# A two-layer decoder step: memory attention ahead of the HGRN heads, both sample heads of a pair in one step, twelve gates behind them

## The chip, the cores and the metric

One Trainium2 chip, one of its cores. TensorE (PE in the profile), VectorE (DVE), ScalarE (ACT), GpSimd (POOL) and the DMA queues run in parallel, each engine in its own order, and wait for each other by semaphores. The metric is the device time of one execution in microseconds (us); lower is better. The time before the change is the median of three runs.

## What is computed

264 tokens (256 of a prompt, 8 samples that each have caches of their own) go through two layers of width 2048. The second layer, where nearly all of the change lies, is this, cut from the reference:

```python
q, f, iv, mq, g = split(x @ w_in)              # 12 + 12 + 12 + 4 + 16 blocks of 128 columns
fg = lb + (1 - lb) * sigmoid(f)                # forget gate
qh, kh, vh = silu(q), 1 - fg, iv
# per head: prompt in chunks, each sample with its own state
state = fg * state + outer(kh, vh);  o = qh @ state
o = o * rsqrt(mean(o**2) + eps) * norm_w
mem = softmax(mq @ mem_k.T / sqrt(128)) @ mem_v    # 4 heads; samples use cache_mem_k, cache_mem_v
y = (concat(o, mem) * silu(g)) @ w_out
x = layer_norm(alpha * x + y)
```

The first layer has sliding-window attention in place of the twelve recurrent heads, and the same memory heads, gates, output projection and norm.

## The kernel before

**The stream.** All that is read in large pieces goes through one list of units (`Stream`, L58 to L131). A unit is a weight block of 128 output columns, or a cache or state block; nearly all are 128 partitions by 2048 numbers in float32, 1 MB. For each unit SyncE (SP) issues a load into one of 4 raw tiles; ACT writes the high float16 half of each number (L97) and DVE the low half, the rest (L98), into one of 4 tiles `hl`; then the unit's function runs. Up to 4 units are split ahead. A raw tile comes free when it has been split; a state tile (`whole=True`) stays, since the new state is computed in it and stored from it.

**A projection** (`proj`, L307) is 48 matmuls: 16 chunks c of the contraction, each in three passes (`passes`, L302 to L305): high weight by high input, high by low, low by high. Each has 264 columns. They add up in one PSUM bank of the tag `pj`, of which there are two; two banks each exist of `pt` and `sc`, one each of `pv` and `ms`.

**Side work.** The attention of a head and the chunkwise recurrence of a pair of heads (`hg_side`, L1064) are generators in a queue. After each unit `after` (L1278) calls `pump(1)`: the first generator in the queue runs one step. For a pair the steps are: diagonal products `hd`; products for the spans 1, 2, 4, 8, 16, 32, 64 (`hs`, masked into `st`); transposes `pk` and updates `pu`; the output `hpo`; square and mean (`rms`, L1182); log and exponential (L1183, L1186) for the reciprocal root; the scaled result (L1189). What is written here is the order of issue; a scheduler then sets each engine's order by a model of its own, so that side work stands between the matmuls of projections. At run time every engine keeps that order.

**Layer two**, as it stands in the list: for each of six pairs of heads the blocks f, f, v, v, q, state, q, state, where a state unit is one head (half a tile, L1197 to L1243: sample output `hos`, then eight updates of the state by ACT L1237 and DVE L1238, each with a product `vb` from PE, then a store from POOL's queue, L1241). For heads 0 to 7 (`NG1`) the gate block g comes right behind its state unit. Then four blocks mq, four blocks of the memory key cache and four of the value cache (`ck_unit`, `cv_unit`, each 32 very small matmuls, with the softmax `mems_soft` between them), gates 8 to 15 among and behind them, then the 16 blocks of the output projection (`o`). A gate unit (`gate_unit`) computes silu; `gate_by` (L727) multiplies it into the head's result and splits the product into the tile `mix`, chunk j, which is what the output projection reads. The output projection's first unit first drains the side queue (`out_unit`, L767).

In the first layer the first q block follows the block of keys and values `kv`, which holds both `pj` banks (and both `sc`) until L249, L251 and their neighbours have read them; in the same way the first f block of layer two follows `mv`.

Of the kernel before, what the change touches and what calls it, by code (L numbers as in the profile page):

```python
# [18 lines left out]
P = 128  # L19
# [14 lines left out]
NG1 = 8  # L34
# [23 lines left out]
class Stream:  # L58


    def __init__(self, nc, pool, nraw, nsplit):
        self.nc, self.pool = nc, pool
        self.nraw, self.nsplit = nraw, nsplit
        self.units = []
        self.raw = {}
        self.hl = {}

# [16 lines left out]
    def prep(self, i):  # L84
# [9 lines left out]
        for k, s in enumerate(self.parts(i)):  # L94
# [10 lines left out]
    def run(self, pump):  # L105
# [11 lines left out]
        for i in range(n):  # L117
# [8 lines left out]
            while free < prepped and (free <= i or self.units[free][5]):  # L126
                free += 1
# [7 lines left out]
def trunk_kernel(  # L135
# [75 lines left out]
    bias_s = pm.tile([P, 2, NQ], F32, name="bias_s")  # L211

# [770 lines left out]
    def f_unit(h):  # L983
        def fn(hl):
# [4 lines left out]
            pt = proj(hl, xhl, T, f"f{h}")  # L989
            i = h % 2  # L990
            if i == 0:
# [3 lines left out]
                cur["ks8"] = p1.tile([P, 2, TS], F32, tag="ks8", name=f"ks8{h}", bufs=2)  # L995
            fg, kk, ks8 = cur["fg"][:, i], cur["kk"][:, i], cur["ks8"][:, i]
# [6 lines left out]
            nc.vector.tensor_scalar_mul(ks8, kk, 1.0 / (SA * SK))  # L1003
# [5 lines left out]
    def hq_unit(h):  # L1009
        def fn(hl):  # L1010
# [5 lines left out]
            if h % 2 == 1:  # L1016
                side.append(hg_side(h // 2, cur["q"], cur["vn"], cur["fg"], cur["qk"]))
# [23 lines left out]
    def hv_rows(h, vt, vs, vn, vr):  # L1041
# [7 lines left out]
        nc.vector.tensor_copy(vr[:, i], p16)  # L1049
# [14 lines left out]
    def hg_side(pi, q, vn, fg, qk):  # L1064
# [119 lines left out]
        for i, sq in enumerate(sqs):  # L1184
# [3 lines left out]
            scaled = mix[:, h] if h >= NG1 else sq  # L1188
# [3 lines left out]
            if h < NG1:  # L1192
                gate_by(sq, mix[:, h], h)
# [3 lines left out]
    def state_unit(h):  # L1197
        def fn(hl):
            p1 = H["p"]
            pi, i = h // 2, h % 2  # L1200
            raw = stream.raw[state_at[h]][:, : TS * P]
            R = raw.rearrange("p (b v) -> p b v", b=TS)
            v = hl[:, :, : TS * P].rearrange("p s (b v) -> p s b v", b=TS)
            vr, fgs, ks8 = cur["vr"][:, i], cur["fg"][:, i, TP:T], cur["ks8"][:, i]
            qs, vts = (cur[n][:, i, TP:T] for n in ("q", "vt"))
            ks = cur["kk"][:, i]
            if i == 0:
                osb[pi] = p1.tile([P, 2, T], F32, tag="osb", name=f"osb{pi}", bufs=2)
            qk = p1.tile([P, TS], F32, tag="qk", name=f"qk{h}", bufs=2)
            qf = p1.tile([P, TS], F32, tag="qf", name=f"qf{h}", bufs=2)  # L1210
            qfh = p1.tile([P, TS, 2], F16, tag="qfh", name=f"qfh{h}", bufs=2)
            nc.vector.scalar_tensor_tensor(qf, qs, SA * 0.5 * CP, fgs, op0=ALU.mult, op1=ALU.mult)
            nc.vector.scalar_tensor_tensor(qk, qs, 8.0 * 0.5 * CP / SK, ks, op0=ALU.mult, op1=ALU.mult)
            qkh = p1.tile([P, 2, TS], F16, tag="qkh", name=f"qkh{h}", bufs=2)
            nc.scalar.activation(qkh[:, 0], qk, AF.Copy)
            nc.vector.tensor_tensor(qkh[:, 1], qk, qkh[:, 0], op=ALU.subtract)
            nc.scalar.activation(qfh[:, :, 0], qf, AF.Copy)
            nc.vector.tensor_tensor(qfh[:, :, 1], qf, qfh[:, :, 0], op=ALU.subtract)
            po = bank("ms", 1, f"hos{h}")
            pov = po[:, : 2 * TS].rearrange("p (b s) -> p b s", s=2)  # L1220
            for b in range(TS):
                mm(pov[:, b], v[:, 0, b], qfh[:, b], start=True, stop=False)
                mm(pov[:, b, 0:1], v[:, 1, b], qfh[:, b, 0:1], start=False, stop=True)
# [49 lines left out]
    while late:  # L1273
        g1(late.popleft())
# [158 lines left out]
```

## Time and profile before

| | us |
|---|---|
| median of three runs | 906.5 (905.1 to 909.17) |
| the profiled execution | 906.08 |
| its span, first to last instruction | 904.3 |
| PE busy in the span | 886.6 |
| DVE busy | 701.5 |
| ACT busy | 582.4 |

Layer two's f block begins at 420.1 us of the span, its caches at 729 us, its output projection at 800 us. In the rows of the profile, a line such as `PE hpo L1169 <- ACT st L1147: 1.5, 1, 1.5` says that PE, about to run the instruction of line 1169 that writes `hpo`, stood idle for 1.5 us, once, until ACT had done line 1147, which writes `st`. In a table of windows each engine's number is its busy time in that stretch, with the number of its instructions; PEclk is the granted TensorE clock, 1.00 being full. A matmul's time in the timeline holds its way through the array: two of them overlap, so that matmuls of 264 columns start 0.11 us apart and each lasts 0.28.

### The profile page before, as it was taken

What the parts mean: (1) busy time and instruction counts of PE and PEld (TensorE: products, weight loads), DVE (VectorE), ACT (ScalarE), POOL (GpSimd) and SP (SyncE); (2) the same over time, 40 slices, a digit from 0 to 9 for tenths busy, and PEclk for the clock granted to TensorE, in tenths of its full rate; (3) what the DMA queues carried; (4) which work ended last, traced back from release to release, by engine and by line L of the source; (5) the groups of instructions that cost most, each with busy time, mean ns of one, the idle gap of its engine ahead of it and who ended that gap; (6) DMA issues with size and microseconds to landing.
All of it is one profiled execution on the core that took longest, in us unless ns stands there. A gap on an engine that the chain in (4) does not pass through costs nothing.

```text
span 904.3 us, 21814 instructions
## 1 busy us (share of the span) xinstructions
PE 886.6 (98%) x9281; PEld 762.9 (84%) x9281; DVE 701.5 (78%) x1230; ACT 582.4 (64%) x982; POOL 34.9 (4%) x68
## 2 busy tenths in 40 slices
PE   9999999999999999999999999999999999799996
PEld 6888889678888888876888888898888888688996
DVE  6879877669886666697687887979788989678736
ACT  6767776657664444476766877777777585858415
POOL 1100010000000000002000000000000000000000
PEclk9999999999999999999999999999999999899999
DMA  9998566557785555556374655827454878456303
GB/s 340 392 353 317 188 245 209 188 208 265 262 333 192 187 192 203 207 198 214 127 292 137 216 201 174 299 101 260 160 215 164 303 283 308 172 207 244 130 2 97
DMA packets 37853, 198.67 MB, mean 220 GB/s; under 512 B 4555, under 2 KB 10732, under 8 KB 17532
## 3 DMA queue, kind: packets, MB, share of 16 engines
q1 hardware_dynamic: 33024, 181.55, 56.3%
q0 software_dynamic: 4688, 15.67, 4.6%
q8 instruction: 72, 1.18, 0.5%
q14 instruction: 25, 0.20, 0.1%
q10 hardware_dynamic: 44, 0.07, 0.0%
HBM read 180.03 MB, written 17.22 MB: 218 GB/s over the span
## 4 chain that ended last, share of the span: by engine, by line
PE 77%; DVE 8%; ACT 6%; DMA 6%; issue 3%; SPq 0%; ACTq 0%; DVEq 0%
PE o L303 5%; PE o L305 5%; PE o L304 5%; PE g L305 5%; PE g L303 5%; PE g L304 5%; DVE hl L98 4%; ACT hl L97 2%; PE hv L305 2%; PE hv L303 2%; PE hv L304 2%; DMA raw<-in_w_in 2%; PE hq L303 2%; PE hq L305 2%; PE hq L304 2%
## 5 line engine op out<-in xcount | busy, mean ns | idle before, releaser
L98 DVE SCALAR_TENSOR_TENSOR hl<-raw,hl 128x2048 f16<-128x2048 f32 (+2 forms) x168 | 358.6, 2138 | 82.0 <-ACT hl L97 81.0
L97 ACT ACTIVATE hl<-raw 128x2048 f16<-128x2048 f32 (+2 forms) x168 | 299.2, 1784 | 97.8 <-PE o L305 45.4
L305 PEld LDWEIGHTS <-hl 128*128 128x128 f16 (+2 forms) x2048 | 197.4, 98 | 31.8 <-DVE hl L98 2.9
L303 PEld LDWEIGHTS <-hl 128*128 128x128 f16 (+2 forms) x2048 | 197.3, 98 | 30.6 <-issue 2.2
L304 PEld LDWEIGHTS <-hl 128*128 128x128 f16 (+2 forms) x2048 | 197.4, 98 | 30.3 <-issue 2.2
L305 PE MATMUL g<-xhl,hl 128*128 128x264 f16 x512 | 142.0, 277 | 2.4 <-DVE hl L98 2.4
L303 PE MATMUL g<-xhl,hl 128*128 128x264 f16 x512 | 141.9, 277 | 0.0
L304 PE MATMUL g<-xhl,hl 128*128 128x264 f16 x512 | 141.9, 277 | 0.0
L303 PE MATMUL o<-mix,hl 128*128 128x264 f16 x384 | 105.4, 276 | 0.8 <-DVE xres L747 0.8
L304 PE MATMUL o<-mix,hl 128*128 128x264 f16 x384 | 105.8, 276 | 0.0
L305 PE MATMUL o<-mix,hl 128*128 128x264 f16 x384 | 105.7, 276 | 0.0
L303 PE MATMUL q<-xhl,hl 128*128 128x264 f16 x192 | 53.0, 276 | 1.0 <-DVE kst L251 1.0
L303 PE MATMUL f<-xhl,hl 128*128 128x264 f16 x192 | 52.9, 276 | 0.4 <-DVE mvhl L251 0.4
L305 PE MATMUL hv<-xhl,hl 128*128 128x264 f16 x192 | 53.0, 276 | 0.0
L303 PE MATMUL hq<-xhl,hl 128*128 128x264 f16 x192 | 53.0, 276 | 0.0
L304 PE MATMUL hq<-xhl,hl 128*128 128x264 f16 x192 | 53.0, 276 | 0.0
L305 PE MATMUL hq<-xhl,hl 128*128 128x264 f16 x192 | 53.0, 276 | 0.0
L304 PE MATMUL hv<-xhl,hl 128*128 128x264 f16 x192 | 53.0, 276 | 0.0
L303 PE MATMUL hv<-xhl,hl 128*128 128x264 f16 x192 | 53.0, 276 | 0.0
L304 PE MATMUL q<-xhl,hl 128*128 128x264 f16 x192 | 53.0, 276 | 0.0
L305 PE MATMUL q<-xhl,hl 128*128 128x264 f16 x192 | 53.0, 276 | 0.0
L304 PE MATMUL f<-xhl,hl 128*128 128x264 f16 x192 | 52.9, 276 | 0.0
(338 smaller groups left out, 1858.4 us busy)
## 6 DMA issues: line engine op xcount, KB each, us to landing
raw<-in_w_in SPq DMA_DIRECT2D x88, 1024.0 KB, 6.4
raw<-in_w_o SPq DMA_DIRECT2D x32, 1024.0 KB, 5.0
raw<-in_w_mk SPq DMA_DIRECT2D x8, 1024.0 KB, 4.9
raw<-in_w_mv SPq DMA_DIRECT2D x8, 1024.0 KB, 4.9
raw<-in_c_mk SPq DMA_DIRECT2D x8, 1024.0 KB, 5.1
raw<-in_c_mv SPq DMA_DIRECT2D x8, 1024.0 KB, 7.0
raw<-in_state SPq DMA_DIRECT2D x12, 512.0 KB, 5.4
out_ss<-raw POOLq DMA_DIRECT2D x12, 512.0 KB, 5.5
```

Source lines behind the costliest of these rows:

```text
L97: hi = self.nc.scalar.activation(hl[:, 0, s], raw[:, s], AF.Copy, scale=scale)
L98: lo = self.nc.vector.scalar_tensor_tensor(hl[:, 1, s], raw[:, s], scale, hl[:, 0, s], op0=ALU.mult, op1=ALU.subtract)
L303: mm(out, lhs(0), rhs(0), start=start, stop=False)
L304: mm(out, lhs(0), rhs(1), start=False, stop=False)
L305: return mm(out, lhs(1), rhs(0), start=False, stop=stop)
```

## The change

- **Memory attention first.** Layer two begins f0, the four mq, and then the eight cache blocks with f1, v0, v1, q0, g0, g1, q1, f2, f3 between them. Before, the caches stood behind all six pairs.
- **Joint sample steps.** One state unit per pair, 1 MB, behind both q blocks. The sample work of both heads goes in one set of instructions. The state update of the first head is issued with the unit, that of the second head one unit later; the raw tile is held for one unit longer (`longer`).
- **Gates.** Only 0, 1, 2 and 6 stand among the pairs. The other twelve come behind the last pair: 3, 4, 5, 7, 8, 9, 12 to 15, then 10 and 11.
- **Pumping.** After a unit two steps are run while more than one side job is queued, and none or two at places in a small table.
- **Pieces.** The units of layer two up to the output projection are split in two pieces of 1024 columns.
- **`apart`.** For q0 of layer one and f0 of layer two the passes with the high weight run first for all 16 chunks, those with the low weight behind them, in the bank `pv`.
- The factor that turned `kk` into `ks8` (L1003) moves into the constant `sel`. `LATER` is empty, so that the code for updates still later does not run.

```diff
-NG1 = 8
+EARLY = (0, 1, 2, 6)
+LATER = ()
...
-        for k, s in enumerate(self.parts(i)):
+        for k, s in enumerate((slice(0, 1024), slice(1024, 2048)) if i in self.halved else self.parts(i)):
...
-            while free < prepped and (free <= i or self.units[free][5]):
+            while free < prepped and (free + self.longer.get(free, 0) <= i or self.units[free][5]):
...
+        if apart:
+            pt = bank("pv", 1, name)
+            for k, (c, s, r) in enumerate([(c, 0, r) for c in range(NC) for r in range(2)] + [(c, 1, 0) for c in range(NC)]):
+                mm(pt[:, :n], w[:, s, c], src[:, r, c, cols], start=k == 0, stop=k == 3 * NC - 1)
+            return pt[:, :n]
...
-            pt = proj(hl, xhl, T, f"q{j}")
+            pt = proj(hl, xhl, T, f"q{j}", apart=j == 0)
...
-            pt = proj(hl, xhl, T, f"f{h}")
+            pt = proj(hl, xhl, T, f"f{h}", apart=h == 0)
...
-            nc.vector.tensor_scalar_mul(ks8, kk, 1.0 / (SA * SK))
...
+            def half(i):
+                update(2 * pi + i, R[:, i], vr[:, i, : P // 2].bitcast(F16), fgs[:, i], ks[:, i], H["sel"])
+
+            half(0)
+            later.append(lambda: half(1))
...
+    f_of(0)
+    for h in range(NM):
+        w1("mq", h, mem1_sides(mq_unit(h)) if h == NM - 1 else mq_unit(h))
+    cache(c_mk, ck_unit, 0)
+    f_of(1, 2)
...
+    cache(c_mv, cv_unit, 3)
+    f_of(3)
+    state_of(0)
...
+    for pi in range(2, HD // 2):
+        for of in (f_of, v_of):
+            of(2 * pi)
+            of(2 * pi + 1)
+        q_of(2 * pi)
+        q_of(2 * pi + 1)
+        state_of(pi)
+        if 2 * pi in EARLY:
+            gate_of(2 * pi)
+    last = (HD - 2, HD - 1)
...
+    for k, j in enumerate([j for j in range(NC) if j not in EARLY and j not in last] + list(last)):
+        w1("g", j, fetch_first(gate_unit(1, j)) if k == 6 else gate_unit(1, j))
+    stream.halved = range(n_first, len(stream.units))
...
-        pump(1)
+        pump(pumps[i] if i in pumps else 2 if len(side) > 1 and i > state_at[0] else 1)
```

What this does to the engines' orders is shown at two places. The first is PE at the end of the last pair of heads (heads 10 and 11): `hs_64` is its last span, `pk`, `hpo` and `pu` its transposes, output and update, `rms` the means of squares. Before, `mrow`, `mback` and `mso` (the memory softmax of the samples and the value cache) stand among them:

```order
L305 MATMUL hs_64_10507<-qk_2_5655 128x64
L1152 MATMUL pk_10521<-ident,qk_10_9379 128x128 x4
L1169 MATMUL hpo_10636<-st_10088,vn_9535 128x128
L1170 MATMUL hpo_10636<-st_10088,vn_9535 128x128
L1158 MATMUL pu_10565<-vn_9535,kn_10526 128x128 x4
L666 MATMUL mrow_10687<-ident,mst_10685 32x128 x2
L1171 MATMUL hpo_10636<-qk_10_9379,s_10570 128x128
L1169 MATMUL hpo_10636<-st_10088,vn_9535 128x128
L1170 MATMUL hpo_10636<-st_10088,vn_9535 128x128
L1171 MATMUL hpo_10636<-qk_10_9379,s_10570 128x128
L677 MATMUL mback_10698<-ident,mrows_10690 128x32 x2
L1182 MATMUL rms_10704<-osq_10644,ones_rms 128x264
```

In the changed kernel, the same steps (lines 1161 to 1191 there; `o_0_11311` and `o_0_11369` are the first two blocks of the output projection, L308 the first of its passes):

```order
L310 MATMUL hs_64_10878<-qk_2_5663 128x64
L1161 MATMUL pk_10892<-ident,qk_10_9767 128x128 x4
L1178 MATMUL hpo_11034<-st_10419,vn_9968 128x128
L1179 MATMUL hpo_11034<-st_10419,vn_9968 128x128
L1167 MATMUL pu_10961<-vn_9968,kn_10897 128x128 x4
L1180 MATMUL hpo_11034<-qk_10_9767,s_10966 128x128
L1178 MATMUL hpo_11034<-st_10419,vn_9968 128x128
L1179 MATMUL hpo_11034<-st_10419,vn_9968 128x128
L1180 MATMUL hpo_11034<-qk_10_9767,s_10966 128x128
L1191 MATMUL rms_11108<-osq_11042,ones_rms 128x264
L1191 MATMUL rms_11111<-osq_11044,ones_rms 128x264
L308 LDWEIGHTS hl_11118
```

The last row is the weight load for chunk 10 of the first output block. Ahead of `hs_64` and the last spans stand 30 matmuls of each of the two output blocks, their chunks 0 to 9; the two blocks fill both `pj` banks. Before, what followed `rms` was the value cache's 256 small matmuls and gates 14 and 15 (with parts of 13).

The second place is ACT in the same stretch. Before, with `mrows` and `msphl` from the memory softmax among the last pair's steps, and the split of a weight tile behind them:

```order
L672 ACTIVATE mrows_10690,mrz_10692<-mrow_10687,mrnm_10691 32x256
L1173 ACTIVATE osb_9734<-hpo_10636 128x2x256
L1177 ACTIVATE osq_10644<-osb_9734 128x264
L1177 ACTIVATE osq_10646<-osb_9734 128x264
L249 ACTIVATE msphl_10701<-mback_10698 128x64
L1183 ACT_TABLE_LOAD
L1183 ACTIVATE osq_10644<-rms_10704,eps_rms 128x264
L1183 ACTIVATE osq_10646<-rms_10707,eps_rms 128x264
L1186 ACT_TABLE_LOAD
L1186 ACTIVATE osq_10644<-osq_10644 128x264
L1186 ACTIVATE osq_10646<-osq_10646 128x264
L97 ACTIVATE hl_10975<-raw_10717 128x2048
```

In the changed kernel, where the two rows `mix<-sil` are the high halves of the gated results of heads 10 and 11:

```order
L1171 ACTIVATE s_10966<-pu_10961 128x256
L1182 ACTIVATE osb_10261<-hpo_11034 128x2x256
L1186 ACTIVATE osq_11042<-osb_10261 128x264
L1186 ACTIVATE osq_11044<-osb_10261 128x264
L1192 ACT_TABLE_LOAD
L1192 ACTIVATE osq_11042<-rms_11108,eps_rms 128x264
L1192 ACTIVATE osq_11044<-rms_11111,eps_rms 128x264
L1195 ACT_TABLE_LOAD
L1195 ACTIVATE osq_11042<-osq_11042 128x264
L1195 ACTIVATE osq_11044<-osq_11044 128x264
L739 ACTIVATE mix<-sil_11232 128x264
L739 ACTIVATE mix<-sil_11292 128x264
```

The steps of the last pair are the same and in the same order; the memory softmax's are gone from between them, and behind the exponentials stand at once the two copies that the output projection's chunks 10 and 11 read.

More of the change, by code (lines that the diff above doesn't have):

```diff
@@ L66, in __init__ @@
         self.hl = {}
+        self.halved = range(0)
+        self.longer = {}
     def add(self, src, fn, scale=SW, pre=None, split=True, whole=False, home=None):
@@ L1195, in hg_side, with update @@
         yield
-    def state_unit(h):
+    def update(h, R, vr, fgs, ks, sel):
+        for g in range(2):
+            pvb = bank("pt", 2, f"vb{h}{g}")
+            for bb in range(4):
+                mm(pvb[:, bb * P : (bb + 1) * P], sel[:, 4 * g + bb], vr, start=True, stop=True)
+            for bb in range(4):
+                b = 4 * g + bb
+                s = R[:, b]
+                nc.scalar.activation(s, s, AF.Copy, scale=fgs[:, b : b + 1])
+                nc.vector.scalar_tensor_tensor(
+                    s, pvb[:, bb * P : (bb + 1) * P], ks[:, b : b + 1], s, op0=ALU.mult, op1=ALU.add
+                )
+        nc.gpsimd.dma_start(ss_o[h // 2, :, h % 2 * TS * P : (h % 2 + 1) * TS * P], R.rearrange("p b v -> p (b v)"))
@@ L1201, in fn @@
[L1201 to L1209, printed above, removed]
@@ L1210, in fn @@
-            qf = p1.tile([P, TS], F32, tag="qf", name=f"qf{h}", bufs=2)
-            qfh = p1.tile([P, TS, 2], F16, tag="qfh", name=f"qfh{h}", bufs=2)
+            raw = stream.raw[state_at[pi]]
+            v = hl.rearrange("p s (i b v) -> p s i b v", i=2, b=TS)
+            L = left.pop(pi)
+            vr, fgs, ks = L["vr"], L["fg"][:, :, TP:T], L["kk"]
+            qs, vts = (L[n][:, :, TP:T] for n in ("q", "vt"))
+            osb[pi] = p1.tile([P, 2, T], F32, tag="osb", name=f"osb{pi}", bufs=2)
@@ L1215, in fn @@
[L1215 to L1223, printed above, removed]
@@ L1224, in fn @@
-            pq = po[:, 2 * TS : 3 * TS]
+            qkh = p1.tile([P, 2, 2, TS], F16, tag="qkh", name=f"qkh{pi}", bufs=2)
+            split_from(qfh[:, :, :, 0], qfh[:, :, :, 1], qf, 1.0)
+            split_from(qkh[:, 0], qkh[:, 1], qk, 1.0)
+            po = bank("ms", 1, f"hos{pi}")
+            pov = po[:, : 4 * TS].rearrange("p (i b s) -> p i b s", i=2, s=2)
+            for i in range(2):
+                for b in range(TS):
+                    mm(pov[:, i, b], v[:, 0, i, b], qfh[:, i, b], start=True, stop=False)
+                    mm(pov[:, i, b, 0:1], v[:, 1, i, b], qfh[:, i, b, 0:1], start=False, stop=True)
@@ L1259, in mem1_sides, with state_of, gate_of, cache @@
+    def state_of(pi):
+        at = state_at[pi] = len(stream.units)
+        whole = 2 * pi not in LATER
+        if whole:
+            stream.longer[at] = 1
+        stream.add(state[pi], state_unit(pi), SA, whole=whole)
+    def gate_of(h, n=None):
+        w1("g", h, early_gate(h) if h in EARLY else gate_unit(1, h), n)
+    def cache(c, unit, t):
+        pumps[len(stream.units)] = 0
+        stream.add(c[1, t], unit(1, t), SA)
     def mem1_sides(fn):
         return with_side(fn, [lambda h=h: memp_side(1, h) for h in range(NM)])
-    u = stream.units[-1]
@@ L1263, in trunk_kernel, with f_of @@
[L1263 to L1274 removed]
+    def f_of(h, n=None):
+        w1("f", h, f_unit(h), n)
```

142 lines of the change are left out of this document (93 added, 49 removed).

## Prediction

> **What bounds the kernel now.** I read the page's busy times first, then its slices:
>
> ```profile
> PE 886.6 (98%) x9281; PEld 762.9 (84%) x9281; DVE 701.5 (78%) x1230; ACT 582.4 (64%) x982; POOL 34.9 (4%) x68
> PE   9999999999999999999999999999999999799996
> PEclk9999999999999999999999999999999999899999
> ```
>
> PE is the bound: it idles for 904.3 - 886.6 = 17.7 us. The change removes next to no matmul, so it can win only idle time and clock. Both show one dent, in slice 35 of 40. The table of PE's waits names what ends the idle times, and the table of windows places them:
>
> ```profile
> PE g L305 <- DVE hl L98: 2.4, 2, 1.7
> PE hpo L1169 <- ACT st L1147: 1.5, 1, 1.5
> PE q L303 <- DVE kst L251: 1.0, 1, 1.0
> PE mback L677 <- DVE mrows L674: 1.0, 1, 1.0
> PE f L303 <- DVE mvhl L251: 0.4, 1, 0.4
> ```
>
> ```profile
> 205.00:260.00 55.00, 55.00 (x665) 48.57 (x663) 49.00 (x60) 38.38 (x49) 0.00 (x0) 1.00 0.76 275
> 450.00:660.00 210.00, 209.73 (x2246) 185.88 (x2244) 175.95 (x334) 151.84 (x273) 5.90 (x11) 1.00 0.57 199
> 670.00:760.00 90.00, 89.96 (x1043) 79.85 (x1042) 81.68 (x140) 66.16 (x98) 2.14 (x4) 1.00 0.75 270
> 760.00:800.00 40.00, 34.50 (x394) 28.69 (x392) 32.70 (x54) 27.56 (x48) 0.54 (x1) 0.91 0.62 230
> ```
>
> From 450 to 760 PE loses 0.3 us in all. From 760 to 800 it idles 40 - 34.5 = 5.5 us, and its mean clock of 0.91 takes another 40 x 0.09 = 3.6 us. This is where the recurrence's last pair and the samples' memory softmax, two chains of small dependent steps, meet with nothing but two gates left. The clock falls behind the gaps:
>
> ```profile
> 770.00:772.00 2.00, 0.53 (x4) 0.53 (x5) 0.82 (x1) 1.90 (x3) 0.00 (x0) 1.00 0.59 234
> 776.00:778.00 2.00, 1.86 (x34) 1.57 (x34) 0.23 (x1) 1.97 (x4) 0.00 (x0) 1.00 0.95 393
> 778.00:780.00 2.00, 1.76 (x19) 1.31 (x19) 0.00 (x0) 1.97 (x4) 0.00 (x0) 0.53 0.05 21
> 780.00:782.00 2.00, 2.00 (x41) 1.68 (x40) 1.67 (x4) 2.00 (x3) 0.00 (x0) 0.61 0.03 8
> ```
>
> **Stage 760 to 800: -9.1 us.** The change takes the caches and the memory attention out of this stage and puts twelve gates behind the last pair. What they meet at the front of layer two is what layer one has already: eight cache blocks between projections, in the window 205 to 260, with PE busy for 55.0 of 55 us at 275 GB/s. So I cost the move itself at nothing. Its cover is the projections between the caches; their eight loads of 1 MB move with them on SP's queue, past state and weight loads, and 275 GB/s were had there. Without cover it would cost the 1.0 us that `mback` waits now. The 5.5 + 3.6 us go; late next is the last pair's own chain.
>
> **The new wait: +6.3 us.** In the changed order PE runs the last spans (`hs_64`) only behind chunks 0 to 9 of the first two output blocks. Then `pk`, `hpo`, `pu`, `rms`, and next chunk 10, which needs head 10's gated result. Both `pj` banks are taken, so that no third block can start. Twelve gates do not cover this: they run before it. Its length is read from the same chain before, in the timelines of ACT, DVE and PE (start, duration, engine, line, operation, what it writes and reads, count):
>
> ```profile
> 771.06 0.36 ACT L1147 ACTIVATE st<-hs 64x256 f32<-64x256 f32 x1
> 774.93 0.57 ACT L1173 ACTIVATE osb<-hpo 128x512 f32<-128x512 f32 x1
> 775.53 0.73 ACT L1177 ACTIVATE osq<-osb 128x264 f32<-128x264 f32 x2
> 776.41 1.28 ACT L1183 ACT_TABLE_LOAD   x1
> 777.71 0.85 ACT L1183 ACTIVATE osq<-rms,eps_rms 128x264 f32<-128x264 f32 x2
> 778.58 1.28 ACT L1186 ACT_TABLE_LOAD   x1
> 779.87 0.73 ACT L1186 ACTIVATE osq<-osq 128x264 f32<-128x264 f32 x2
> 782.31 0.41 ACT L729 ACTIVATE mix<-sil 128x264 f16<-128x264 f32 x1
> ```
>
> ```profile
> 780.33 0.90 DVE L1189 SCALAR_TENSOR_TENSOR mix<-osb,small_t,osq 128x264 f32<-128x264 f32 x2 [3.67 <-ACT osq L1186]
> 781.74 0.77 DVE L728 SCALAR_TENSOR_TENSOR sil<-sil,mix 128x264 f32<-128x264 f32 x2
> ```
>
> ```profile
> 769.31 0.63 PE L1152 MATMUL pk<-ident,qk 128*128 128x128 f32 x4
> 772.02 1.09 PE L1158 MATMUL pu<-vn,kn 128*128 128x128 f32 x8
> 774.35 0.39 PE L1171 MATMUL hpo<-qk,s 128*128 128x128 f32 x2
> 776.01 1.16 PE L1182 MATMUL rms<-osq,ones_rms 128*128 128x264 f32 x4
> ```
>
> From the copy of `st` at 771.06 to the end of the two scalings at 780.33 + 0.90 = 781.23 it is 10.2 us. Behind them the product (about half of 0.77) and the split's high half (0.41) add 0.8; the memory softmax's two steps on ACT and PE, gone from between, take off about 0.3. That makes 10.7 us from `hs_64` to chunk 10. PE's own work in it is `pk` 0.63, `hpo` and `pu` together about 2.6 and `rms` 1.16, 4.4 us in all; idle are 10.7 - 4.4 = 6.3. Bounds: 5.5, if copies and products overlap more, and 8.2, if a weight split of 1.9 us gets between, as it does before the copy of `st` now. Queued behind these steps on DVE and ACT stand the reads of the first output block and the splits of `hl` from the fifth block on; four blocks are split ahead, of which 36 + 96 matmuls at 0.11 us, 14.5 us, are still to run when chunk 10 is there, so nobody waits for those.
>
> **Clock: +2.0 us.** The wait's last part, from the end of `rms` to chunk 10, is 6.3 less the about 2 us of gaps up to `rms`: 4.3 us with PE empty. The rows at 778 and 780 lost 2 x 0.47 + 2 x 0.39 = 1.7 us behind smaller gaps; I take a little more. Bounds 0 and the 3.6 us of the stage now. The Trainium skill (TensorE: Matmul & The Clock Gate, section "What's actually happening") says that the array drops to half rate after at least one idle window of about 3.4 us and comes back after one busy window. This trace does not bear out the first half: the clock fell at 778 with no wait above 1.5 us before it. By the page the new wait, unlike the old ones, would halve the clock for about 3.4 us, a cost of 1.7 us, and the sum would come to 903.8, an estimate.
>
> **`apart`: -1.4 us.** q0 of layer one waits 1.0 us and f0 of layer two 0.4 for a `pj` bank (rows above); in `pv` they need not. Each could give nothing, if a later wait takes it up; then the sum is 1.4 higher.
>
> **Pieces, joint step, `ks8`: +0.2 us.** The prices of splits by form, of a gate's product, and of the small product with the ones:
>
> ```profile
> L98 DVE SCALAR_TENSOR_TENSOR hl<-raw,hl 128x2048 f16<-128x2048 f32 x146 | 333.9, 2291 | 73.9 <-ACT hl L97 73.2
> L97 ACT ACTIVATE hl<-raw 128x2048 f16<-128x2048 f32 x146 | 277.8, 1906 | 92.2 <-PE o L305 45.4 <-DMA raw<-in_w_in 11.5 <-PE mv L593 10.2
> L98 DVE SCALAR_TENSOR_TENSOR hl<-raw,hl 128x1024 f16<-128x1024 f32 x18 | 22.0, 1220 | 3.4 <-ACT hl L97 3.1
> L97 ACT ACTIVATE hl<-raw 128x1024 f16<-128x1024 f32 x18 | 18.9, 1051 | 2.6 <-DMA raw<-in_w_kv 2.6
> L728 DVE SCALAR_TENSOR_TENSOR sil<-sil,mix 128x264 f32<-128x264 f32 x24 | 10.3, 431 | 2.4 <-ACT mix L634 1.9
> L1226 PE MATMUL hos<-qkh,ones x24: 166/166/167, 452.4 to 717.1; 128*128 128x8 f16 x24
> ```
>
> Two pieces cost 2 x 1.22 - 2.29 = 0.15 us on DVE and 2 x 1.05 - 1.91 = 0.20 on ACT; DVE idles for 34 us of 450 to 660, so this hides. Twelve fewer of the ones products save PE between 0 and 12 x 0.166 = 2.0; overlapped as they are, I take 0.3. For waits on the smaller steps that I can't see I add 0.5 (0 to 3). The joint state tile is held longer, and a later weight load on SP's queue waits for its store:
>
> ```profile
> raw<-in_w_in SPq DMA_DIRECT2D x88, 1024.0 KB, 6.4
> out_ss<-raw POOLq DMA_DIRECT2D x12, 512.0 KB, 5.5
> ```
>
> Store, load and split take 5.5 + 6.4 + 3.4 = 15 us. In the changed order some five to six projections lie between the last update and the block whose load waits, at 264 columns each, 48 x 0.11 = 5.4 us a block: about 30 us. That covers it; otherwise the price would be the part above 30.
>
> **Sum.** 906.08 - 9.1 + 6.3 + 2.0 - 1.4 + 0.2 = 904.1, against this execution; the median of the three runs, 906.5, is 0.4 above it. I say 904.0. The wait is not removed but exchanged for another of nearly its size.
>
> **Rivals.** *The clock holds and the wait is short* (0.31): 906.08 - 9.1 + 5.5 - 1.4 - 0.3 = 900.8. For it: PE has run 350 us without a gap when the wait comes, and the stage now has six breaks where the new one has about four. Against it: the rows at 778 and 780. *DVE becomes the bound in the pairs* (0.14), slower: now a pair takes 210 / 4 = 52.5 us, DVE busy for 44.0 and idle for 8.5 of them. A gate gone from a pair takes 5.4 us from PE, but from DVE only 2.29 + 3 x 0.43 = 3.6. A pair with no gate is 41.7 us of PE and 44.0 - 7.2 + 7 x 0.15 = 37.9 of DVE. If DVE still lost 8.5 us per pair to its own waits, that would be 46.4: 2.35 us for each of the four gates that leave pairs 1 to 3, 9.4 us, giving 913.5. It decides once DVE's idle time per pair stays above 3.8 us. Against it: the window 670 to 760 is mostly without gates, DVE is at 81.68 of 90, and PE does not wait. *The exchange is even, or the first two steps bring nothing* lies inside my forecast (0.55): up to 907.5.
>
> **How the numbers follow.** About 0.5%, 4.5 us, is what a measurement of this kernel can tell from no change: faster is below 902.0, slower above 911.0. The fast rival lies at 899 to 902, the slow one at 911 to 916; my forecast's own bounds are 901.5 to 907.5. Faster 0.32, within 0.53, slower 0.15. The range is 899 to 911, leaving out the slow rival and the last of the fast one.
>
> **What would show it.** Right: PE idle behind `rms` of the last pair, 5 to 8 us in four or so pieces, ended by ACT's L739; half clock behind it; no idle for `mback` or for `hl` in gates; q0 and f0 without a wait; PE full up to the first output block. Wrong: PE waits for `hl`, `hs` or `vb` products in the pairs, or the last chain's wait below 4 us, or new waits among the caches.

## The result and the profile after

The changed kernel takes 914.9 us (median of four runs, 913.6 to 918.4) against 906.3 us of the kernel before on the same chip: ratio 1.0098, 95% interval 1.0079 to 1.0117. It is slower by 1.0%, outside the range of 899 to 911. The profiled execution took 915.42 us, its span is 913.6.

The page after, first its busy times, then the slices of PE and of its clock (40 slices of 22.8 us):

```profile
PE 889.9 (97%) x9269; PEld 764.2 (84%) x9269; DVE 699.0 (77%) x1240; ACT 586.8 (64%) x1034; POOL 34.9 (4%) x68
...
PE   9999999999999999999999999989998999979996
...
PEclk9999999999999999999999999999999999989998
```

There was one dent; now there are three, near 600, 700 and 815 us. PE idles for 913.6 - 889.9 = 23.7 us, 6.0 more than before. The table of PE's waits names what ends them:

```profile
PE hpo L1178 <- ACT st L1156: 6.2, 2, 3.1
PE o L308 <- ACT mix L739: 4.8, 1, 4.8
...
PE rms L1191 <- ACT osq L1186: 1.1, 1, 1.1
...
PE hpo L1180 <- ACT s L1171: 0.5, 1, 0.5
```

The waits for `hl`, `mback`, `kst` and `mvhl` are gone. The windows of the pairs, of the first of their two dents, of the old dent and of the new end (PE's busy time comes first after the length, the granted clock third from the right):

```profile
440.00:800.00 360.00, 352.12 (x3830) 309.92 (x3828) 301.19 (x570) 260.20 (x491) 9.12 (x17) 0.99 0.59 213
600.00:620.00 20.00, 16.85 (x156) 14.43 (x155) 14.14 (x36) 13.59 (x35) 1.07 (x2) 0.91 0.33 121
...
760.00:800.00 40.00, 39.84 (x403) 34.81 (x401) 36.15 (x71) 24.67 (x38) 1.61 (x3) 1.00 0.59 210
800.00:830.00 30.00, 23.61 (x193) 18.98 (x191) 12.36 (x19) 15.89 (x23) 0.54 (x1) 0.89 0.25 89
```

The old dent is closed (39.84 of 40 us). The end idles for 30 - 23.61 = 6.4 us, the forecast's 6.3, and loses 30 x 0.11 = 3.3 us of clock, against 2.0. The miss lies in the first row: 7.9 us idle in the pairs, and the clock lost behind their two dents (20 x 0.09 = 1.8 us in the one shown), where before only 0.3 us was lost between 450 and 760.

The first of the two waits for `st`, in the timelines of PE, ACT and DVE (start, duration, engine, line, operation, count):

```profile
606.60 0.38 PE L1054 MATMUL hvp<-ident,hvt 128*128 128x128 f32 x2
610.08 0.49 PE L1178 MATMUL hpo<-st,vn 128*128 128x128 f32 x2 [3.09 <-ACT st L1156]
```

```profile
602.03 0.62 ACT L1088 ACTIVATE qk<-qk 128x512 f16<-128x512 f32 x1
603.08 4.78 ACT L1214 ACTIVATE raw<-raw,fg 128x128 f32<-128x128 f32 x16 [0.43 <-DVE hl L102]
607.77 1.99 ACT L101 ACTIVATE hl<-raw 128x1024 f16<-128x1024 f32 x2
609.66 0.36 ACT L1156 ACTIVATE st<-hs 64x256 f32<-64x256 f32 x1
```

```profile
608.84 2.36 DVE L102 SCALAR_TENSOR_TENSOR hl<-raw,hl 128x1024 f16<-128x1024 f32 x2 [2.79 <-ACT hl L101]
```

With the pairs counted from 0, PE has the last span of pair 1 ready at about 606. Its copy into `st` stands on ACT behind sixteen scalings of pair 3's sample states (both heads at once, 4.78 us) and a weight split. DVE idles for 2.8 us of this time, until that split comes. The second such wait is at 702 us: the copy of pair 3 behind the scalings of pair 5.

### The profile page after: what moved, and what is told of

Its sections match the earlier page's. It is cut to its first block, busy times and chain, and to the rows that moved or that the text cites. A ratio compares the mean times of both kernels' runs of the same rounds, so it can differ in the third digit from the quotient of the medians.

```text
span 913.6 us, 21829 instructions
## 1 busy us (share of the span) xinstructions
PE 889.9 (97%) x9269; PEld 764.2 (84%) x9269; DVE 699.0 (77%) x1240; ACT 586.8 (64%) x1034; POOL 34.9 (4%) x68
## 4 chain that ended last, share of the span: by engine, by line
PE 83%; DVE 8%; ACT 6%; issue 1%; ACTq 0%
PE o L308 6%; PE o L309 6%; PE o L310 6%; PE g L308 6%; PE g L309 6%; PE g L310 6%; DVE hl L102 4%; PE q L309 2%; PE q L310 2%; PE q L308 2%; ACT raw L1214 2%; PE hq L309 2%; PE hq L310 2%; PE hq L308 2%; PE mq L309 2%; PE mq L310 2%
## 5 line engine op out<-in xcount | busy, mean ns | idle before, releaser
L102 DVE SCALAR_TENSOR_TENSOR hl<-raw,hl 128x1024 f16<-128x1024 f32 (+2 forms) x232 | 364.9, 1591 | 79.9 <-ACT hl L101 78.9
L101 ACT ACTIVATE hl<-raw 128x1024 f16<-128x1024 f32 (+2 forms) x232 | 304.3, 1345 | 80.9 <-PE o L310 48.7
L308 PEld LDWEIGHTS <-hl 128*128 128x128 f16 (+2 forms) x2016 | 194.7, 98 | 34.8 <-issue 5.5
L309 PEld LDWEIGHTS <-hl 128*128 128x128 f16 (+2 forms) x2016 | 194.8, 98 | 29.8 <-issue 1.7
L310 PEld LDWEIGHTS <-hl 128*128 128x128 f16 (+2 forms) x2016 | 194.8, 98 | 28.8 <-issue 0.2
L308 PE MATMUL g<-xhl,hl 128*128 128x264 f16 x512 | 141.4, 276 | 0.2 <-DVE sil L744 0.2
L308 PE MATMUL o<-mix,hl 128*128 128x264 f16 x384 | 106.8, 279 | 4.8 <-ACT mix L739 4.8
L309 PE MATMUL o<-mix,hl 128*128 128x264 f16 x384 | 107.1, 279 | 0.0
L310 PE MATMUL o<-mix,hl 128*128 128x264 f16 x384 | 107.1, 279 | 0.0
L308 PE MATMUL hq<-xhl,hl 128*128 128x264 f16 x192 | 54.1, 282 | 0.0
L309 PE MATMUL hq<-xhl,hl 128*128 128x264 f16 x192 | 54.1, 282 | 0.0
L310 PE MATMUL hq<-xhl,hl 128*128 128x264 f16 x192 | 54.0, 281 | 0.0
L308 PE MATMUL hv<-xhl,hl 128*128 128x264 f16 x192 | 53.0, 276 | 0.0
L309 PE MATMUL q<-xhl,hl 128*128 128x264 f16 x176 | 48.6, 276 | 0.0
L310 PE MATMUL q<-xhl,hl 128*128 128x264 f16 x176 | 48.6, 276 | 0.0
L308 PE MATMUL q<-xhl,hl 128*128 128x264 f16 x176 | 48.6, 276 | 0.0
L310 PE MATMUL f<-xhl,hl 128*128 128x264 f16 x176 | 48.6, 276 | 0.0
L309 PE MATMUL f<-xhl,hl 128*128 128x264 f16 x176 | 48.6, 276 | 0.0
```

The costliest lines, as they stand in the source:

```text
L101: hi = self.nc.scalar.activation(hl[:, 0, s], raw[:, s], AF.Copy, scale=scale)
L102: lo = self.nc.vector.scalar_tensor_tensor(hl[:, 1, s], raw[:, s], scale, hl[:, 0, s], op0=ALU.mult, op1=ALU.subtract)
L308: mm(out, lhs(0), rhs(0), start=start, stop=False)
L309: mm(out, lhs(0), rhs(1), start=False, stop=False)
L310: return mm(out, lhs(1), rhs(0), start=False, stop=stop)
```

## The experiments

Three theories. *ACT's queue*: the joint step's scalings hold up the recurrence's small steps on ACT. *Short pairs*: without a gate, DVE has too much to do in a pair. *Late gates*: the end's wait belongs to the twelve gates put last.

### One head at a time

The joint step is undone: 12 units of half a tile again, each behind its head's q block.

```diff
-        q_of(2 * pi)
-        q_of(2 * pi + 1)
-        state_of(pi)
+        for h in (2 * pi, 2 * pi + 1):
+            q_of(h)
+            state_of(h)
...
-            half(0)
-            later.append(lambda: half(1))
+            update(h, raw.rearrange("p (b v) -> p b v", b=TS), vr, fgs, ks, H["sel"])
```

> The changed kernel with its joint sample step undone: a state unit and its eight updates for one head at a time again, behind that head's q block; caches first, the twelve late gates, pumping, pieces and apart stay as changed. Queue theory (the sixteen state scalings of the joint step, 4.7 us in a row on ACT, stand ahead of the copy of st that PE waits for, twice 3.1 us, and push the recurrence's steps back so far that the last pair has no gates left over it): both waits for st fall below 1 us each and the last pair's rms stands among the gates, 914.9 - 12 - 9.8 + 1 to 3 = 894 to 897 us. Short-pair theory (pairs without a gate are too short for what DVE has to do in them, whatever the sample step): the 12 us of the pairs stay, 903 to 915. Late-gate theory (the last chain's wait belongs to putting the gates last): the pairs' 12 us go, the wait of 5 us for mix at the first output block stays, 902 to 905.

905.1 us, ratio 0.9977 (0.9962 to 0.9992). Its windows and two of its waits, PE's and ACT's:

```profile
440.00:800.00 360.00, 352.38 (x3877) 310.35 (x3875) 304.87 (x620) 268.42 (x514) 9.66 (x18) 1.00 0.60 213
...
800.00:830.00 30.00, 30.00 (x269) 26.09 (x268) 19.86 (x20) 16.50 (x15) 0.00 (x0) 1.00 0.65 238
```

```profile
PE hs L308 <- ACT qk L1088: 3.8, 6, 1.0
PE hq L308 <- DVE vs L256: 1.8, 1, 1.8
```

```profile
ACT hl L101 <- DMA raw<-in_w_in: 19.2, 14, 5.2
```

No theory met it in full. *Late gates* is refuted: the gates stand last as before, and the end's wait is gone. *Queue* is right on that and on the waits for `st`, but 8 us out in the time. *Short pairs* has the time in its range, and the pairs idle for as long as before, 7.6 us, though in small waits at a full clock. Part of these is of another kind: ACT now waits 19.2 us for weight loads between 440 and 800 (1.8 in the changed kernel). That a pair's two half states take two of the four raw tiles may be the reason; no run tests it, and the kernel before, with the same half tiles, waits 6.7 us there.

### No scaling

```diff
-                nc.scalar.activation(s, s, AF.Copy, scale=fgs[:, b : b + 1])
```

> The changed kernel without the scaling of the sample states on ACT (the state's decay is left out of the new state, 96 instructions of 0.29 us); all else stays. Queue theory: with nothing between hs and the copy of st on ACT, PE's waits for st fall below 1 us each, and the last pair's steps come earlier in PE's order, 893 to 897 us. Short-pair theory: DVE has just as much to do, 912 to 916 us. Late-gate theory: 902 to 905.

The new sample state is left without its decay here. 894.8 us, 0.9851 (0.9831 to 0.9870), as the queue theory had it.

```profile
440.00:800.00 360.00, 359.54 (x3954) 318.97 (x3953) 310.71 (x586) 242.17 (x412) 9.65 (x18) 1.00 0.61 220
800.00:830.00 30.00, 30.00 (x274) 26.12 (x273) 23.03 (x23) 19.76 (x16) 0.00 (x0) 1.00 0.71 257
```

Both losses go with 28.8 us of ACT's work, while DVE's work is the same. It shows where, not yet how. One head at a time has as many scalings, so that this run alone does not price the joint step.

### Both halves one unit later

```diff
-            half(0)
+            later.append(lambda: half(0))
...
-            stream.longer[at] = 1
+            stream.longer[at] = 2
```

> The changed kernel with both halves of the joint state update issued one unit later, the raw tile held one unit longer; the same instructions, and on ACT the copies of st now stand ahead of the sixteen scalings or between them. The last chain stands as in the changed kernel, behind chunk 9 of the first two output blocks. Queue theory: the two waits of 3.1 us for st and the clock lost behind them go, 902 to 906 us, and the wait of about 5 us for mix stays. Short-pair theory: 912 to 917, since no engine has less to do. A raw tile held longer could cost loads: then PE would wait for hl.

914.7 us, 1.0083 (1.0063 to 1.0102): nothing gained.

```profile
PE o L308 <- ACT mix L739: 4.8, 1, 4.8
PE hs L308 <- ACT qk L1088: 4.1, 8, 0.7
```

The two long waits for `st` are gone, and eight short ones for `qk` have come in their place. Which copy the scalings stand in front of is not the point.

### No pieces

```diff
-    stream.halved = range(n_first, len(stream.units))
```

> The changed kernel with its weight blocks of layer two split in one piece of 2048 columns again. Queue theory: the scalings and one split of 1.9 us still stand ahead of st, 912 to 916 us, waits for st of 2 to 4 us. Short-pair theory: DVE has 0.15 us and ACT 0.2 us less per block, seven blocks a pair, some 4 to 5 us over four pairs where DVE is the bound, 909 to 912 us.

925.9 us, 1.0206 (1.0182 to 1.0230): both theories said nothing or a small gain. Whole splits make the pairs idle for 15.6 us:

```profile
440.00:800.00 360.00, 344.36 (x3732) 304.06 (x3731) 290.95 (x496) 251.28 (x421) 9.12 (x17) 0.98 0.58 211
```

### The scaling on GpSimd, and on DVE

```diff
-                nc.scalar.activation(s, s, AF.Copy, scale=fgs[:, b : b + 1])
+            four = slice(4 * g, 4 * g + 4)
+            nc.gpsimd.tensor_tensor(R[:, four], R[:, four], fgs[:, four].unsqueeze(2).to_broadcast([P, 4, P]), op=ALU.mult)
```

The second kernel has `nc.vector` in place of `nc.gpsimd`; both once for four samples.

> The changed kernel with the scaling of the sample states moved from ACT (96 instructions of 0.29 us) to GpSimd, one multiply of 128x512 for four samples; the new state is computed in full. PE's order becomes that of the run without the scaling, the last pair's rms among the gates. ACT-load theory (ACT's own work of 28 us in the pairs is what the recurrence's steps queue behind, wherever it stands): 894 to 899 us, waits in the pairs below 2 us in all. DVE theory (the pairs lack time on DVE, or GpSimd slows DVE): waits of PE for DVE in the pairs of 5 us and more, 903 to 912.

> The changed kernel with the scaling moved from ACT to DVE, one multiply of 128x512 for four samples, 24 of some 0.6 us: DVE gets about 14 us more, ACT 28 us less. PE's order at the end stays the late one, rms behind chunk 9. ACT-load theory: the 12 us of the pairs go, the wait for mix of 5 us stays, 902 to 906 us. DVE theory: DVE is the late one in the pairs already, so they lose 14 us more or a good part of it, 916 to 925 us.

GpSimd: 906.4 us, 0.9988 (0.9969 to 1.0008), in the range of the DVE theory, which allowed for GpSimd slowing DVE. The end is covered, but the pairs idle for 8.2 us, of which PE waits 4.9 for ACT's `qk` and 2.8 for DVE's. DVE: 908.1 us, 1.0009 (0.9988 to 1.0030), above the one theory's 902 to 906 and far below the other's 916 to 925. The pairs' loss halves, the end keeps its own (this kernel runs the end some 8 us earlier):

```profile
440.00:780.00 340.00, 336.13 (x3706) 297.41 (x3704) 304.06 (x579) 227.38 (x387) 9.14 (x17) 1.00 0.61 219
780.00:820.00 40.00, 33.60 (x309) 28.27 (x308) 22.00 (x34) 21.95 (x30) 0.54 (x1) 0.91 0.34 113
```

DVE got 15 us more to do and the kernel became faster: DVE was not the late engine in the pairs of the changed kernel.

### Gates 4 and 8 back in their pairs

```diff
-EARLY = (0, 1, 2, 6)
+EARLY = (0, 1, 2, 4, 6, 8)
```

> The changed kernel with gates 4 and 8 back behind the sample steps of their pairs (a gate is 5.4 us of PE), ten gates last; the joint step stays. On ACT the copies of st stand ahead of the scalings or behind two of them. Short-pair theory: the pairs have room again and lose at most 3 us instead of 12, the last chain starts two gates later in PE's order (the span 16 too stands behind chunk 9 of the first output blocks) and waits 3 to 4 us longer, 905 to 909 us. ACT-load theory: the load of a pair on ACT is not less, the waits move, 911 to 917 us.

909.6 us, 1.0029 (1.0010 to 1.0048), just above the range of the short-pair theory. Two gates' room cures most of the pairs' idle time, with ACT's load unchanged; the end grows by 1.4 us and keeps half clock for longer:

```profile
440.00:780.00 340.00, 338.40 (x3713) 299.67 (x3711) 288.32 (x552) 255.64 (x482) 9.14 (x17) 1.00 0.61 218
780.00:820.00 40.00, 32.23 (x283) 26.46 (x281) 22.73 (x35) 18.90 (x28) 0.55 (x1) 0.83 0.34 128
```

### One head at a time, with gates 0 to 7

The first kernel, with the gates 3, 4, 5 and 7 back as well.

```diff
-EARLY = (0, 1, 2, 6)
+EARLY = (0, 1, 2, 3, 4, 5, 6, 7)
```

> The changed kernel with the joint step undone and gates 0 to 7 back among the pairs, eight gates last: what is left of the change is the caches first, the pieces, apart and the pumping. Short-pair theory: pairs lose 1 to 3 us as before the change; the last pair's rms stands behind chunk 9 of the first output blocks, a wait of about 5 us for mix and some clock, 900 to 905 us. ACT-load theory: the same, since ACT has one head's scalings at a time and a gate's 5.4 us of PE to run them beside; it differs from the run with one head at a time and late gates, 905.1 us, only by where the waits stand.

908.2 us, 1.0014 (0.9992 to 1.0037), slower than expected: the pairs still idle for 3.7 us (ACT waits 12 us for loads), and the end is uncovered again, with 4.8 us for `mix`.

### The end alone: two more output blocks in PE's order

```diff
-                out_part(l, i, hl, slice(0, T))
+                out_part(l, i, hl, slice(0, T), "pt" if l and 2 <= i < 4 else "pj")
```

The second kernel has the scaling on DVE besides, as above.

> The changed kernel with the third and fourth output block of layer two in the two pt banks, so that 60 more matmuls of their chunks 0 to 9 (6.8 us) stand in PE's order between the last pair's pu and chunk 10; nothing else. Late-gate theory, as the prediction had it (the end costs 6.4 us of waits and some 3 us of clock because no third block can start): the wait for mix falls from 4.8 us to below 1, 914.9 - 6.8 - 2 = 905 to 908 us, and the waits of 3.1 us for st stay. Rival (the end's wait is covered by the clock coming back later, or ACT and DVE are held up by the residuals of four blocks): 911 to 915.

> Both repairs: the scaling on DVE (908.1 us alone) and the two output blocks in the pt banks. If the two losses are separate, they add: 908.1 - 7 to 9 = 899 to 901 us, faster than both kernels. If one only uncovers the other (PE arrives earlier at the last chain and waits longer for it): 904 to 907.

911.6 us, 1.0052 (1.0033 to 1.0071), and 904.5 us, 0.9978 (0.9965 to 0.9990). Each gains some 3.5 us, half of what was hoped for, and lies in the range of its rival (911 to 915; 904 to 907). The trace of the second shows why:

```profile
800.00:830.00 30.00, 26.53 (x222) 22.21 (x220) 11.01 (x19) 16.03 (x22) 0.54 (x1) 0.94 0.21 75
```

The idle time falls from 6.4 to 3.5 us. In the timeline `hpo`'s part that reads `s` starts 4.4 us behind the first one (807.03 against 802.64); without the filling it is 2.3 us. The filling stands on PE ahead of the chain's own steps and delays what it is to cover.

### One head at a time with gates 4 and 8; the same with the scaling on DVE

```diff
 # both: the kernel of the first experiment, and
-EARLY = (0, 1, 2, 6)
+EARLY = (0, 1, 2, 4, 6, 8)
 # the second besides
-                nc.scalar.activation(s, s, AF.Copy, scale=fgs[:, b : b + 1])
+            nc.vector.tensor_tensor(R[:, four], R[:, four], fgs[:, four].unsqueeze(2).to_broadcast([P, 4, P]), op=ALU.mult)
```

> The changed kernel with the joint step undone (905.1 us alone, waits of 9 us in the pairs, none at the end) and gates 4 and 8 back in pairs 2 and 4. PE's order keeps the last pair's rms inside gate 11, ahead of the output projection. Short-pair theory: the pairs get room, their waits fall from 9 to 3 or 4 us, and the end waits 0 to 2 us: 898 to 902. ACT-load theory in its narrow form (only the bunch of sixteen hurts): no bunch is there any more, so nothing is gained, 904 to 906.

> As the run before, and the scaling on DVE: ACT has 28 us less, DVE 14 us more. Short-pair theory with ACT as the late engine: another 1 to 3 us, 896 to 901. If by then DVE is the late one: 902 to 906.

The first: 900.3 us, 0.9927 (0.9911 to 0.9943), faster than both kernels. Pairs idle for 5.2 us, the end for 0.6. The second, 905.0 us, 0.9985 (0.9973 to 0.9997), loses most of it again. Here ACT has 23 us less to do between 440 and 800, and its longest wait is for a load:

```profile
526.07 2.00 ACT L101 ACTIVATE hl<-raw 128x1024 f16<-128x1024 f32 x2 [4.86 <-DMA raw<-in_w_in]
527.98 0.61 ACT L1088 ACTIVATE qk<-qk 128x512 f16<-128x512 f32 x1
```

The split whose load is late stands in front of `qk`, for which PE waits 2.5 us. The range foretold for a late DVE, 902 to 906, holds the time, but of PE's 8.5 us of waits in the pairs 8.1 end with ACT. That loads are a second limit with one head at a time fits these rows; no run that changes the loads alone shows it.

### The scalings twice

```diff
                 nc.scalar.activation(s, s, AF.Copy, scale=fgs[:, b : b + 1])
+                nc.scalar.activation(s, s, AF.Copy, scale=1.0)
```

> The changed kernel with every scaling of the sample states done twice on ACT, the second time by 1.0: another 96 instructions of 0.29 us, 28 us; DVE has nothing more. ACT-load theory: the pairs, which lose 12 us with 28 us of scalings and next to nothing without, lose clearly more, 922 to 935 us, and ACT is what PE waits for. DVE or plain order theory (the loss hangs on where the planner puts the steps, or on DVE): 912 to 919.

916.8 us, 1.0113 (1.0096 to 1.0130), in the range for order or DVE (912 to 919) and 5 us below the one for ACT's load. Pairs idle for 8.1 us, hardly more than the 7.9 of the changed kernel, though ACT has 17.6 us more to do in them:

```profile
440.00:800.00 360.00, 351.95 (x3816) 309.77 (x3814) 300.64 (x570) 277.76 (x586) 9.14 (x17) 0.99 0.60 215
```

So the loss is not in proportion to ACT's load. The scheduler moved copies of `st` ahead of scalings: the one of pair 1 runs at 607.22 us now, the next scalings from 610.46.

### The pieces alone, in the kernel before

```diff
+        self.halved = range(0)
...
-        for k, s in enumerate(self.parts(i)):
+        for k, s in enumerate((slice(0, 1024), slice(1024, 2048)) if i in self.halved and self.units[i][0].shape[1] == 2048 else self.parts(i)):
...
+    stream.halved = range(n_first, len(stream.units))
```

> The kernel before, with nothing but the weight blocks of layer two split in two pieces of 1024. In the changed kernel, taking the pieces away cost 11 us. If pieces let small steps of the recurrence in between splits in any order of the work: 899 to 904 us here, most of it between 760 and 800, where PE waits 1.5 us for st behind a split. If they pay only where the pairs are short: 905 to 908.

900.6 us, 0.9940 (0.9925 to 0.9955). The stage that the change was to clear, nothing moved:

```profile
440.00:760.00 320.00, 317.67 (x3488) 281.07 (x3487) 276.15 (x565) 234.93 (x445) 9.15 (x17) 1.00 0.60 217
760.00:800.00 40.00, 39.17 (x439) 33.85 (x438) 34.85 (x61) 32.59 (x59) 0.55 (x1) 1.00 0.73 272
```

Idle is 0.8 us instead of 5.5, at a full clock. The 2.3 us among the pairs are seven short waits for `qk`, the longest 0.4.

### The joint step alone, and apart alone, both with the pieces in the old order

```diff
+    for pi in range(HD // 2):
+        for of in (f_of, v_of, q_of):
+            of(2 * pi)
+            of(2 * pi + 1)
+        state_of(pi)
+        for h in (2 * pi, 2 * pi + 1):
+            if h in EARLY:
+                gate_of(h)
...
-        pump(pumps[i] if i in pumps else 2 if len(side) > 1 and i > state_at[0] else 1)
+        pump(1)
```

In the first the caches and gates 8 to 15 stand behind the pairs as before, and q0 and f0 are without apart. The second is the kernel of the last experiment with this:

```diff
-            pt = proj(hl, xhl, T, f"q{j}")
+            pt = proj(hl, xhl, T, f"q{j}", apart=j == 0)
...
-            pt = proj(hl, xhl, T, f"f{h}")
+            pt = proj(hl, xhl, T, f"f{h}", apart=h == 0)
```

> The joint sample step and the pieces alone, in the order of before: pairs with gates 0 to 7 among them, caches behind the pairs, gates 8 to 15 among and behind the caches, one step of side work behind each unit, no apart. Its neighbour is the kernel before with the pieces, 900.6 us. If the joint step costs by itself (sixteen scalings in one bunch on ACT, in every pair): 904 to 910 us, waits for st or qk in the pairs of 4 us and more. If it costs only where the pairs are without gates and the last chain has nothing behind it but the output projection: 899.5 to 902, waits in the pairs as with the pieces alone, 2 to 3 us.

> The kernel before with the pieces (900.6 us) and with apart for q0 and f0. The prediction took 1.4 us for apart: 899.2 us, no wait of PE for kst or mvhl. If a later wait takes it up, as the stretch 100 to 120 us of the changed kernel suggests: 900 to 901.

The joint step alone: 911.4 us, 1.0051 (1.0030 to 1.0072), 10.8 us more than its neighbour of 900.6.

```profile
440.00:760.00 320.00, 317.27 (x3444) 281.36 (x3442) 265.21 (x500) 232.04 (x435) 9.10 (x17) 1.00 0.58 212
760.00:800.00 40.00, 33.18 (x382) 27.34 (x380) 35.38 (x58) 29.01 (x49) 0.54 (x1) 0.89 0.73 267
```

The pairs lose next to nothing more (2.7 us against 2.3). The price is paid at the last chain: 6.8 us idle and 40 x 0.11 = 4.4 us of clock. No scaling stands in front of that chain. The last of them and the last copy of `st` on ACT, and below that copy in the neighbour:

```profile
690.36 4.78 ACT L1214 ACTIVATE raw<-raw,fg 128x128 f32<-128x128 f32 x16
...
780.36 0.36 ACT L1156 ACTIVATE st<-hs 64x256 f32<-64x256 f32 x1
```

```profile
750.42 0.38 ACT L1148 ACTIVATE st<-hs 64x256 f32<-64x256 f32 x1 [0.26 <-PE hs L306]
```

The end of the last pair's chain has come 30 us later, in among the memory softmax, and the scalings were done 85 us before it. PE's longest waits there are 3.0 us for the products with the memory keys (`msc`, behind `ms` on ACT) and 2.1 for `rms`.

With apart: 898.7 us, 0.9914 (0.9895 to 0.9933), the fastest of all. The two intervals overlap, so that the 2.0 us between the medians are not certain. PE's waits for `kst` and `mvhl` are absent in this trace and in that of the pieces without apart, so that no run ties the 2.0 us to them.

### Two steps of side work behind each unit

The joint step takes six units out of the list, and after each unit side work is issued.

```diff
-        pump(pumps[i] if i in pumps else 2 if len(side) > 1 and i > state_at[0] else 1)
+        pump(pumps[i] if i in pumps else 2 if i > state_at[0] else 1)
```

In the kernel with the joint step alone:

```diff
-        pump(1)
+        pump(2 if i > n_first else 1)
```

> The changed kernel with two steps of side work behind every unit from the first state unit on, not only while more than one side job is queued; the joint step stays. The planner then has the last pair's rms inside gate 11, two blocks earlier. Step-count theory (the joint step takes six units out of the list, and with them six places where side work is issued, so that the recurrence falls behind; its own instructions cost little): the end's wait falls from 6.4 us with its clock to 0 to 1, 904 to 908 us, and the waits in the pairs stay near 10 us. ACT-bunch theory (the joint step costs by its sixteen scalings): nothing of that is changed, the pairs wait longer as the steps come closer together, 912 to 918.

> The joint step and the pieces in the old order (911.4 us with one step of side work behind each unit), with two steps behind each unit of layer two. The planner has the last pair's rms 1.1 blocks earlier. Step-count theory: the loss of 12 us between 760 and 800 goes, 900 to 904 us, near the 900.6 of the pieces with one head at a time. ACT-bunch theory: 909 to 913.

913.4 us, 1.0081 (1.0066 to 1.0096), and 908.2 us, 1.0024 (1.0012 to 1.0036). The first:

```profile
440.00:800.00 360.00, 347.84 (x3795) 305.86 (x3793) 299.08 (x571) 259.47 (x490) 9.66 (x18) 0.99 0.58 211
800.00:830.00 30.00, 30.00 (x265) 26.05 (x263) 18.79 (x21) 20.41 (x25) 0.00 (x0) 1.00 0.47 163
```

The end is covered now, and the pairs idle for 12.2 us instead of 7.9. The waits went from the end to the pairs; `vb` waits 5.6 us for the update on DVE. In the second, the last copy of `st` is back at 758.68 us, and a wait of 4.9 us of the memory keys for `hl` replaces the old ones; its time lies between the two theories' ranges, and 7.6 of the 10.8 us stay. Steps issued sooner do not make the joint step cheap.

## Why the prediction was wrong

**Stage 760 to 800, -9.1: right in size, wrong in what it takes.** 5.5 us idle and 3.6 of clock went, as 39.84 of 40 us at clock 1.00 show. But the pieces alone, without any move, take nearly all of it (0.8 us idle left, at a full clock), so that beside them the move had next to nothing left to win.

**The new wait, +6.3: right.** 0.5 + 1.1 + 4.8 = 6.4 us behind `hpo`, `rms` and chunk 10, ended by ACT's L739. The chain from the copy of `st` to chunk 10 was put at 10.7 us; these rows give 817.83 - 806.84 = 11.0:

```profile
806.84 0.38 ACT L1156 ACTIVATE st<-hs 64x256 f32<-64x256 f32 x1 [4.65 <-PE hs L310]
```

```profile
817.83 0.60 PE L308 MATMUL o<-mix,hl 128*128 128x264 f16 x2 [4.78 <-ACT mix L739]
```

**Clock, +2.0: 3.3, inside its bounds.** The clock falls during the wait and comes back after 822:

```profile
814.00:816.00 2.00, 0.00 (x0) 0.00 (x0) 0.00 (x0) 1.97 (x4) 0.00 (x0) 1.00 0.00 0
816.00:818.00 2.00, 0.17 (x1) 0.10 (x1) 1.77 (x5) 1.00 (x4) 0.00 (x0) 0.52 0.00 0
...
820.00:822.00 2.00, 2.00 (x11) 1.32 (x10) 0.00 (x0) 0.00 (x0) 0.00 (x0) 0.50 0.00 0
822.00:824.00 2.00, 2.00 (x15) 1.57 (x14) 0.43 (x1) 1.10 (x1) 0.00 (x0) 0.78 0.00 0
```

PE, empty since about 813, is at half rate from 816 and, though busy from 817.8, until about 822.9. The Trainium skill (TensorE: Matmul & The Clock Gate, section "What's actually happening") has the array drop after an idle window of about 3.4 us and return after a busy one. In this trace the fall fits it, and the return took some 5 us of busy array. The waits of 3.1 us in the pairs, shorter than that window, cost clock as well (0.91 over 600 to 620).

**Apart, -1.4:** both waits are gone, but they are gone too in the run with the pieces alone; the price of 2.0 us between two medians is not certain.

**Pieces, joint step, `ks8`, +0.2, and the move itself at nothing: here the prediction failed.** It costed the joint step's instructions and its buffers, and covered all else with "for waits on the smaller steps that I can't see I add 0.5 (0 to 3)". Four steps lead from the kernel before to the changed one, one part at a time (the kernel before took 905.8 to 906.7 us on the chips of these runs):

| | us | this part |
|---|---|---|
| the kernel before | 906.1 | |
| pieces | 900.6 | -5.5 |
| apart | 898.7 | -2.0 |
| the new order, its gates and its pumping (one head at a time) | 905.1 | +6.4 |
| joint step: the changed kernel | 914.9 | +9.8 |

The pieces are worth 5.5 us in the old order (906.1 to 900.6) and 11.0 in the new (914.9 to 925.9): small steps on ACT and DVE stand behind splits of half the length. The new order, forecast at -9.1 + 6.3 + 2.0 = -0.8, costs 6.4 beside the pieces, in pairs that have lost their gates: with one head at a time they idle for 2.3 us in the old order, 3.7 with gates 0 to 7 in the new one, 5.2 with 4 and 8 back, 7.6 in the order of the change. The joint step costs 9.8 us in the new order and 10.8 in the old. Its instructions are no more than before. The prediction speaks neither of the sixteen scalings that now stand in one row on ACT nor of the six units fewer behind which side work is issued. Its forecast of 904.0 is also 0.5 below its own sum: 904.1 goes from an execution 0.4 below the median.

*The rival that DVE becomes the bound* gave 913.5, close to the result by luck, for its mechanism was wrong: DVE idles while PE waits for `st`, and 15 us more for DVE made the kernel faster. What was right in it is the condition: a pair without a gate has no room. Two gates back took the pairs from 7.9 us of idle time to 1.6.

What is shown: the joint step costs about 10 us in either order, and most of it at the last chain. In the new order the pairs idle for 7.9 us with it and 7.6 without, the end for 6.4 us (and 3.3 of clock) with it and not at all without. In the old order the end's 0.8 us become 6.8 and 4.4 of clock. With gates 4 and 8 back the joint step costs 9.3 us (900.3 to 909.6), again at the end. In the new order its losses go with the scalings on ACT (without them 20 us less, on DVE 7 less), and two waits of 3.1 us stand directly behind them. What stays open is why the last chain is late. The row of scalings alone does not explain it: none stands ahead of that chain in the old order, and twice the scalings cost only 2 us more. Nor do the missing units alone: two steps behind each unit bring the chain forward, and the waits come up elsewhere.

## What to carry to other kernels

A change of several parts can hide a gain and a loss in one small term: price each part by itself, in the order in which it will stand. An engine that is busy for two thirds of the time can still hold up the bound engine; look in the timeline at what stands in one row ahead of a small step, not only at the engine's share. Before moving large stages to cover a chain of small steps, halve the instructions that these steps queue behind; here that alone took 5.5 us off, while the move beside it cost 6.4. A kernel faster than both came out of it: the old order with pieces and apart, 898.7 us, ratio 0.9914 (0.9895 to 0.9933).

## What the runs showed of the hardware

Work on the idle GpSimd slowed DVE. With the scaling there, the multiply took 1715 ns (times on GpSimd are rough in the profile), and DVE's product of two tensors 796 ns in the mean; both from the groups by line:

```profile
L1212 POOL TENSOR_TENSOR raw<-raw,fg 128x512 f32<-128x512 f32 x24 | 40.5, 1715 | 122.6 <-DVE hl L102 122.5
...
L1089 DVE TENSOR_TENSOR qk<-qk,qk 128x512 f16<-128x512 f32 x42 | 33.4, 796 | 5.2 <-ACT qk L1088 5.1
```

In the changed kernel, and DVE's own multiply of that form in the kernel with the scaling on DVE:

```profile
L1089 DVE TENSOR_TENSOR qk<-qk,qk 128x512 f16<-128x512 f32 x42 | 29.0, 702 | 0.2
```

```profile
L1212 DVE TENSOR_TENSOR raw<-raw,fg 128x512 f32<-128x512 f32 x24 | 15.2, 681 | 0.0
```

In the mean the same instruction became 13% longer, and GpSimd needs 2.5 times as long as DVE. Five of the 42 products take some 1.52 us, more than twice the usual time, and each of them runs beside GpSimd's multiplies. One of the five, during four multiplies, and the next product after them; first GpSimd, then DVE:

```profile
526.37 7.96 POOL L1212 TENSOR_TENSOR raw<-raw,fg 128x512 f32<-128x512 f32 x4
```

```profile
531.91 1.52 DVE L1089 TENSOR_TENSOR qk<-qk,qk 128x512 f16<-128x512 f32 x1
...
535.57 0.69 DVE L1089 TENSOR_TENSOR qk<-qk,qk 128x512 f16<-128x512 f32 x1 [0.70 <-ACT qk L1088]
```

The Trainium skill (GPSIMD Engine Reference, section "Specifications") says that GpSimd shares its SBUF interface with VectorE and contends with instructions that have two SBUF inputs; these rows agree.
